# The last stage of a decoder layer, written in a fixed order: later statistics, kept weights, rows instead of columns

## The chip, the core and the metric

One core of a Trainium2 chip (trn2) runs the kernel. The time is device microseconds (us) of one execution; the figure to forecast is the median of such times. The engines are named as in the profile: PE (TensorE, matmuls), PEld (its weight load), DVE (VectorE), ACT (ScalarE), POOL (GpSimd), SP (SyncE, which issues all DMAs here).

## What is computed

One layer of a decoder on x of 1024 tokens by 1024 channels in f32: two token mixers, a SwiGLU block, and at its end a gated embedding and the final norm. The last stage of the kernel is these lines of the reference:

```python
    gate = jax.nn.sigmoid(rms_norm(x, norm_ple[i]) @ w_ple_gate[i])
    x = x + gate * (p[i] @ w_ple_proj[i])
return rms_norm(x, norm_final)
```

with `rms_norm(x, gain) = x * rsqrt(mean(x * x) + 1e-6) * gain`, the mean over a token's 1024 channels. All of it must hold to f32 accuracy.

## The kernel before

Activations lie transposed: a tile has 128 channels on the partitions and tokens in its columns, so x2 is eight tiles `x2[m]` of 128 x 1024. The tokens are worked in two halves of 512 columns, `hs(1)` first, then `hs(0)`. A product of f32 accuracy is made of three matmuls of rounded parts (`mm3`, L85 to L87): both operands are split into a high part (a cast on ScalarE, L105) and the rest (a subtraction on VectorE, L106). `xs3[m]` are the split tiles of x2 times the gain; `d_e[m]` in DRAM holds p W_pp, computed earlier.

The last stage begins at L996. For each half it makes eight products, one per output tile m: 24 matmuls against the eight `xs3` tiles into one PSUM bank. Each weight tile comes as two DMAs of 256 KB (`piece`), each of which is split (`halves`, a rotation of four pairs). A product is then finished in `finish` (L1011): times inv3 (L1014, DVE), sigmoid (L1015, ACT), times the tile `pe` loaded from d_e (L1016, DVE), added to x2 (L1017, DVE), squared (L596, L599, ACT) and summed into `acc` (L600, DVE).

A norm's factor is made from `acc` in `stat`: matmuls with a vector of ones sum over the partitions (L116), eleven small instructions on VectorE find the inverse root (L119 to L125), a diagonal is formed (L129), and one matmul spreads it over the partitions (`spread`, L141); ScalarE copies that to inv3 or inv4. There are four such factors of 512 tokens' width: inv3 of both halves at the start of the stage, inv4 of half 1, and inv4 of half 0, the last made in two quarters of 256 tokens at the very end.

Weights are loaded and split twice, once for each half. For the last two weight tiles of the second pass the product is made in quarters, `q2` and `q3`. The output of half 1 is scaled on VectorE (L1025) during the second pass; that of half 0 at the end, by the gain on ScalarE (L1055) and by inv4 on GpSimd and VectorE (`times`, L1059).

In this stage a scheduler sets the order of each engine's instructions. The stage before it (the down projection, L949 evacuates its PSUM banks, L109 and L110 make xs3) is written in a fixed order by `tc.manual_schedule`.

Of the kernel before, what the change touches and what calls it, by code (L numbers as in the profile page):

```python
# [43 lines left out]

@with_exitstack
def hybrid_block(ctx, tc, xT, pT, gains, pscale, w_u, w_qk, w_v, w_ga, w_gb, w_pool, w_a, w_b,
                 w_out, w_gate, w_up, w_down, w_pg, w_pp, out):
# [954 lines left out]
    inv4 = pp.tile([P, S], F32, name="inv4")  # L1002

    def ple_gate(m, w, sl):
        pe = pp.tile([P, HALF], F32, name="pe", bufs=3)[:, :sl.stop - sl.start]
        nc.sync.dma_start(pe, d_e[m][:, sl])
        pg = bank()[:, :sl.stop - sl.start]
        whole(pg, w, xs3, sl)
        return pg, pe

    def finish(m, pg, pe, sl):  # L1011
# [8 lines left out]
    def output(sl):  # L1020
        n = sl.stop - sl.start
        for c in range(0, KT, 2):
            o = pp.tile([P, 2 * HALF], F32, name="o", bufs=3)[:, :2 * n].rearrange("p (m n) -> p m n", m=2)
            for m in range(c, c + 2):
                nc.vector.scalar_tensor_tensor(o[:, m - c, :], x2[m][:, sl], gain(3, m), inv4[:, sl],  # L1025
                                               ALU.mult, ALU.mult)
            nc.sync.dma_start(out[c:c + 2, :, sl].rearrange("m p n -> p m n"), o)

    def squares(h):
        for m in range(KT):  # L1030
            square_into(acc, m, hs(h), nc.vector)

    def spread_into(inv, sl, dg):
        nc.scalar.copy(inv[:, sl], spread(psp, dg, (sl.stop - sl.start) // P))


    held = []
    for m in range(KT):
        w = pieces(w_pg[m])
        held.append((m, *ple_gate(m, w, hs(1))))  # L1040
        if m == 0:
            squares(1)
        elif m == 1:
            dg = stat(psp, acc[:, hs(1)], 4, ev())
            squares(0)
        elif m == 2:
            spread_into(inv3, hs(1), dg)
            dg = stat(psp, acc[:, hs(0)], 4, ev())
        elif m == 3:
            spread_into(inv3, hs(0), dg)  # L1050
        while m > 1 and held:
            finish(*held.pop(0), hs(1))

    def scale(m, sl):
        nc.scalar.activation(x2[m][:, sl], x2[m][:, sl], AF.Copy, scale=gain(3, m))  # L1055

    def times(c, n, sl, eng, inv):
        for m in range(c, c + n):
            eng.tensor_mul(x2[m][:, sl], x2[m][:, sl], inv)  # L1059
        nc.sync.dma_start(out[c:c + n, :, sl].rearrange("m p n -> p m n"), x2a[:, c:c + n, sl])  # L1060

    ws = []
    for m in range(KT):
        w = pieces(w_pg[m])
        if m < KT - 2:
            finish(m, *ple_gate(m, w, hs(0)), hs(0))
            scale(m, hs(0))
        else:
            ws.append((m, w))
        if m == 0:  # L1070
            dg = stat(psp, acc[:, hs(1)], 4, ev())
        if m == 1:
            spread_into(inv4, hs(1), dg)
            output(hs(1))
    q2, q3 = slice(0, 2 * P), slice(2 * P, HALF)
    for m, w in ws:
        finish(m, *ple_gate(m, w, q2), q2)
    (m, w), (m1, w1) = ws
    finish(m, *ple_gate(m, w, q3), q3)
    dg = stat(psp, acc[:, q2], 2, ev(2 * P))  # L1080
    finish(m1, *ple_gate(m1, w1, q3), q3)
    nc.scalar.copy(inv4[:, q2], spread(psp, dg, 2))
    dg = stat(psp, acc[:, q3], 2, ev(2 * P))
    for m, _ in ws:
        scale(m, q2)
    for c in (0, 4):
        times(c, 4, q2, nc.gpsimd, inv4[:, q2])
    for m, _ in ws:
        scale(m, q3)
    ps = spread(psp, dg, 2)  # L1090
    nc.scalar.copy(inv4[:, q3], ps)
    times(0, 2, q3, nc.gpsimd, inv4[:, q3])
    times(2, 3, q3, nc.vector, ps)
    times(5, 3, q3, nc.vector, ps)
# [46 lines left out]
```

## Time and profile before

| what | value |
|---|---|
| three runs | 1462.55, 1465.12, 1469.06 us; median 1465.12 |
| the profiled execution | 1468.2 us, span 1466.5 us |
| PE busy in the span | 1424.5 us (97%) |
| DVE, ACT, POOL busy | 1021.8, 630.6, 393.2 us (70%, 43%, 27%) |
| DMA | 221.73 MB, mean 151 GB/s |
| last stage, products of xs3 | 1347.4 to 1448.6 us |

Times in the rows below are microseconds from the start of the span. "busy" counts an engine's own instructions. A row of a timeline gives start, duration, engine, line, operation and names; in brackets stands how long the engine was idle before it and what ended that. Matmuls overlap, so two starts tell more than a duration.

### The profile page before, as it was taken

Reading aid. Unit: us, or ns where it says so; the run is one execution under the profiler, and the core shown is the slowest. Engines: PE = TensorE matmul, PEld = TensorE weight load, DVE = VectorE, ACT = ScalarE, POOL = GpSimd, SP = SyncE. Lnnn points to the kernel's source line nnn. Section 1 sums busy time; section 2 is a strip of 40 time slices with the busy share of each in tenths; the row PEclk is TensorE's granted clock in tenths of the full one; section 3 lists DMA queues with packets and bytes.
Section 4 is the critical chain, followed back from the end, with each engine's and each line's share of the span. In section 5 each row is a group of like instructions: output and inputs, shape, how many; then the busy total and the mean of one; then the engine's idle time right before and its main releaser. Section 6 shows DMA issues by size and latency. Waiting matters only on the chain.

```text
span 1466.5 us, 19073 instructions
## 1 busy us (share of the span) xinstructions
PE 1424.5 (97%) x6538; PEld 1170.6 (80%) x6538; DVE 1021.8 (70%) x1577; ACT 630.6 (43%) x1174; POOL 393.2 (27%) x454
## 2 busy tenths in 40 slices
PE   8999999999999999998899999999999999999995
PEld 7888888888888878886688888888887888887785
DVE  7680358888777777588656666666666777788886
ACT  6130455555555543355444444444443222226453
POOL 5000012333223300014424434444445233320001
PEclk9999999999999999999899999999999999999998
DMA  6131875455442168333234444444448466622352
GB/s 201 55 134 42 269 218 156 133 154 153 132 123 87 58 223 270 111 115 108 86 115 139 156 151 151 152 157 158 158 143 307 169 238 248 258 72 86 106 185 69
DMA packets 100656, 221.73 MB, mean 151 GB/s; under 512 B 10704, under 2 KB 22480, under 8 KB 100560
## 3 DMA queue, kind: packets, MB, share of 16 engines
q1 hardware_dynamic: 100560, 220.52, 45.2%
q8 instruction: 51, 0.84, 0.2%
q14 instruction: 45, 0.37, 0.1%
HBM read 151.80 MB, written 68.68 MB: 150 GB/s over the span
## 4 chain that ended last, share of the span: by engine, by line
PE 82%; DVE 8%; issue 6%; DMA 1%; POOL 1%; ACT 1%; SPq 0%; DVEq 0%; POOLq 0%; ACTq 0%
PE mm L87 25%; PE mm L86 25%; PE mm L85 25%; DVE fail L411 1%; PE pt L429 1%; DVE t L106 1%; DMA xt<-in_xT 1%; DVE wlo L106 1%; PE av L445 1%; PE av L444 1%; PE z L401 1%; PE z L402 1%; DVE ev L607 1%; PE mm L116 0%; PE mm L141 0%
## 5 line engine op out<-in xcount | busy, mean ns | idle before, releaser
L85 PE MATMUL mm<-t,whi 128*128 128x512 f32 x896 | 354.8, 396 | 9.1 <-ACT t L105 4.1
L105 ACT CAST whi<-wraw 128x512 fp32r<-128x512 f32 x316 | 193.8, 620 | 388.3 <-PE mm L86 264.6
L86 PE MATMUL mm<-t,whi 128*128 128x512 f32 x896 | 353.6, 395 | 4.1 <-DVE t L106 4.1
L87 PE MATMUL mm<-t,wlo 128*128 128x512 f32 x896 | 353.3, 395 | 2.0 <-DVE wlo L106 2.0
L106 DVE TENSOR_TENSOR wlo<-wraw,whi 128x512 fp32r<-128x512 f32 x316 | 233.5, 744 | 125.3 <-ACT whi L105 124.2
L85 PEld LDWEIGHTS mm<-t,whi 128*128 128x128 f32 x896 | 169.2, 189 | 53.0 <-ACT t L105 6.0
L86 PEld LDWEIGHTS mm<-t,whi 128*128 128x128 f32 x896 | 169.2, 189 | 43.6 <-DVE t L106 5.6
L87 PEld LDWEIGHTS mm<-t,wlo 128*128 128x128 f32 x896 | 169.1, 189 | 41.1 <-DVE wlo L106 2.8
L85 PE MATMUL mm<-xs,whi 128*128 128x512 f32 x384 | 154.6, 403 | 0.0
L87 PE MATMUL mm<-xs,wlo 128*128 128x512 f32 x384 | 150.3, 391 | 0.0
L86 PE MATMUL mm<-xs,whi 128*128 128x512 f32 x384 | 150.2, 391 | 0.0
L949 DVE TENSOR_TENSOR x<-mm,x 128x512 f32<-128x512 f32 x140 | 96.1, 690 | 42.8 <-PE mm L87 39.4
L106 DVE TENSOR_TENSOR t<-ev,t 128x512 fp32r<-128x512 f32 x91 | 89.9, 1010 | 30.7 <-ACT t L105 30.3
L411 DVE TENSOR_TENSOR_SCAN fail<-fail 128x1024 f32<-128x1024 f32 (+3 forms) x64 | 87.3, 1364 | 27.3 <-POOL fail L409 26.8
L695 POOL TENSOR_TENSOR ws<-wraw 128x512 f32<-128x512 f32 x22 | 29.9, 1357 | 283.5 <-DMA wraw<-in_w_gate 197.8
L105 ACT CAST t<-ev 128x512 fp32r<-128x512 f32 x95 | 57.5, 620 | 81.7 <-DVE ev L740 42.2
L105 ACT CAST ath<-pt 128x256 fp32r<-128x256 f32 (+1 forms) x176 | 54.8, 335 | 69.5 <-PE pt L429 38.8
L87 PEld LDWEIGHTS mm<-xs,wlo 128*128 128x128 f32 x384 | 72.1, 188 | 15.7
L85 PEld LDWEIGHTS mm<-xs,whi 128*128 128x128 f32 x384 | 72.2, 188 | 11.8 <-ACT sg L373 0.2
L86 PEld LDWEIGHTS mm<-xs,whi 128*128 128x128 f32 x384 | 72.3, 188 | 11.5
L409 POOL TENSOR_SCALAR_AFFINE_SELECT fail<-fail 128x128 f32<-128x128 f32 x64 | 20.6, 322 | 226.7 <-ACT fail L407 201.1
L106 DVE TENSOR_TENSOR atl<-pt,ath 128x256 fp32r<-128x256 f32 (+1 forms) x176 | 61.3, 367 | 18.1 <-ACT ath L105 17.8
(212 smaller groups left out, 2629.3 us busy)
## 6 DMA issues: line engine op xcount, KB each, us to landing
d_t<-t SPq DMA_DIRECT2D x36, 512.0 KB, 3.3
t<-d_t SPq DMA_DIRECT2D x36, 512.0 KB, 6.8
d_b<-t SPq DMA_DIRECT2D x27, 512.0 KB, 2.7
t<-d_b SPq DMA_DIRECT2D x27, 512.0 KB, 6.5
wraw<-in_w_gate SPq DMA_DIRECT2D x44, 256.0 KB, 2.7
wraw<-in_w_up SPq DMA_DIRECT2D x44, 256.0 KB, 3.0
wraw<-in_w_down SPq DMA_DIRECT2D x44, 256.0 KB, 5.1
wraw<-in_w_out SPq DMA_DIRECT2D x32, 256.0 KB, 3.1
```

The source lines that it names most:

```text
L85: nc.tensor.matmul(ps, w[0], x[0], start=first, stop=False, skip_group_check=onto)
L86: nc.tensor.matmul(ps, w[0], x[1], start=False, stop=False, skip_group_check=onto)
L87: nc.tensor.matmul(ps, w[1], x[0], start=False, stop=last, skip_group_check=onto)
L105: nc.scalar.copy(hi, src)
L106: (eng or nc.vector).tensor_sub(lo, src, hi)
L401: nc.tensor.matmul(zo, q[:, base:base + P], kh[:, ks], start=True, stop=False)
L402: nc.tensor.matmul(zo, q[:, base:base + P], kl[:, ks], start=False, stop=True)
L409: nc.gpsimd.affine_select(r[:, :P], r[:, :P], [[1, P]], ALU.is_gt, 1.0, base=0, channel_multiplier=-1)
L411: nc.vector.tensor_tensor_scan(r[:, :w], r[:, :w], r[:, :w], 1.0, ALU.mult, ALU.bypass)
L429: nc.tensor.transpose(pt[:, i, :], b[:, (c + i) * P:(c + i + 1) * P], ident)
L695: nc.gpsimd.tensor_add(s1, a21, a22)
L949: nc.vector.tensor_add(xx, ps, xx)
```

## The change

Only the last stage changes, and one helper: `inv_rms` takes a list of accumulators and sums them in PSUM. In the stage:

- Everything is written in one fixed order (`tc.manual_schedule` on all engines).
- The 16 products are numbered j = 0 to 15; j below 8 are tokens 512 to 1023. In the program's round j stand the product j on TensorE, the finishing of product j-1 (of two waiting products in j = 3 and 4), cut into three pieces by generators, and between these pieces the split of the weights of product j+1.
- The statistic of tokens 0 to 511 for inv3 moves from behind the products of m = 2 into product 6, and that of tokens 512 to 1023 stands in product 1, between two of its steps; the statistic for inv4 stands in product 9.
- The weights of m = 4 to 7 are split into tiles that are kept (`kh`, `kl`), so that the second pass loads and splits only m = 0 to 3.
- For tokens 0 to 511 no inv4 is spread. Their finished tiles are transposed on TensorE (`tokens`, 32 matmuls of 128 x 128), so that tokens lie on the partitions, and the eviction multiplies each row by its factor (`tokens_out`, five on ScalarE and three on VectorE). They go to a second output, `out_1`; the host puts both together.

```diff
+    wkp = ctx.enter_context(pool("wkp"))
+    KEEP = KT // 2
...
+    def prep(j, c):
+        m = j % KT
+        if j not in w:
+            w[j] = kept.get(m, [])
+        if len(w[j]) == 2:
+            return
+        raw = raws[j][c]
+        if m < KEEP:
+            pair = halves(raw)
+        else:
+            pair = [wkp.tile([P, HALF], F32R, name=f"{n}{m}{c}") for n in ("kh", "kl")]
+            split(*pair, raw)
+            kept.setdefault(m, w[j])
+        w[j].append(pair)
...
+    def finish(m, ps, pe, sl, sq=None):
...
+        nc.vector.tensor_mul(a, ps, inv3[:, sl])
         nc.scalar.activation(a, a, AF.Sigmoid)
+        yield
         nc.vector.tensor_mul(a, pe, a)
         nc.vector.tensor_add(x2[m][:, sl], x2[m][:, sl], a)
...
+        nc.scalar.activation(sq, x2[m][:, sl], AF.Square)
+        if sl.start < HALF:
+            nc.scalar.activation(x2[m][:, sl], x2[m][:, sl], AF.Copy, scale=gain(3, m))
+        yield
+        if 0 < m and not (m == KT - 1 and sl.start < HALF):
+            nc.vector.tensor_add(acc[:, sl], acc[:, sl], sq)
+        yield
...
+                nc.tensor.transpose(ps_of[t, m // 4][:, m % 4 * P:(m % 4 + 1) * P],
+                                    x2[m][:, t * P:(t + 1) * P], ident)
...
+        hooks = {1: {4: stat_at(31, acc[:, hs(1)], 4)}, 2: {1: spread_at(31, inv3[:, hs(1)])},
+                 6: {4: stat_at(30, acc[:, hs(0)], 4)}, 7: {1: spread_at(30, inv3[:, hs(0)])},
+                 9: {3: stat_at(41, acc[:, hs(1)], 4)}, 10: {1: spread_at(41, inv4)}}
+        for j in range(14):
+            m, sl = j % KT, hs(1 if j < KT else 0)
+            if j == 1:
+                squares(1, range(1, KT))
+            load_pe(j)
+            ps = products(j, sl, hooks.get(j, {}))
...
+            if j > 2:
+                todo = [waits.pop(0) for _ in range(min(len(waits), 2))]
+            f = [finish(*t) for t in todo]
+            waits.append((m, ps, pes[j], sl))
+            do(*f)
+            prep(j + 1, 0)
+            do(*f)
+            prep(j + 1, 1)
+            do(*f)
+            if 2 < j < 6:
+                squares(0, range(*((0, 3), (3, 6), (6, KT))[j - 3]))
+            if j + 3 < 2 * KT:
+                load(j + 3)
+            if j > 10 and j < 14:
+                output(((0,), (2,), (4, 6))[j - 11])
```

In the changed kernel the lines of a finish are L1049 (times inv3), L1050 (sigmoid), L1052 (times pe), L1053 (added to x2), L1056 (square), L1058 (gain) and L1061 (into acc); L1071 to L1075 are the squares of x2 before the stage, L118 and L122 to L132 the statistic, L144 the spread, L1086 the transposes, L1093 and L1095 the evictions.

Three places of the order follow. First ScalarE in the first pass, before. The names with `whi` are weights (the number before the half tells the raw tile: 12686 belongs to product 6, 12727 and 12733 to product 7), `ev_12528` to `ev_12625` are products 2 to 4.

```order
L1015 ACTIVATE ev_12528<-ev_12528 128x512
L105 CAST whi_12688<-wraw_12686 128x512
L599 ACTIVATE ev_12533<-x2_5854 128x512
L1015 ACTIVATE ev_12578<-ev_12578 128x512
L105 CAST whi_12729<-wraw_12727 128x512
L599 ACTIVATE ev_12583<-x2_5854 128x512
L1015 ACTIVATE ev_12625<-ev_12625 128x512
L105 CAST whi_12735<-wraw_12733 128x512
```

The same place on ScalarE now: `ev_12644` is product 4, `ev_12721` product 5; `kh60` and `kh61` are the halves of the weights of product 6, `kh70` and `kh71` of product 7; L1074 squares x2 for the statistic of tokens 0 to 511.

```order
L1050 ACTIVATE ev_12644<-ev_12644 128x512
L105 CAST kh60_12647<-wraw_12549 128x512
L1056 ACTIVATE ev_12653<-x2_5854 128x512
L105 CAST kh61_12655<-wraw_12551 128x512
L1074 ACTIVATE ev_12660<-x2_5854 128x512
L1074 ACTIVATE ev_12663<-x2_5854 128x512
L1050 ACTIVATE ev_12721<-ev_12721 128x512
L105 CAST kh70_12724<-wraw_12613 128x512
L1056 ACTIVATE ev_12730<-x2_5854 128x512
L105 CAST kh71_12732<-wraw_12615 128x512
```

Between the sigmoid of product m and its square stood a cast for product m+4 before; now a cast for product m+2 stands there, and the second one behind the square.

Second, VectorE at the first statistic of the stage, before: the subtractions that make the low weights of product 3 (`wlo_12539`, `wlo_12545`) and two additions into acc.

```order
L106 TENSOR_TENSOR wlo_12539<-wraw_12536,whi_12538 128x512
L600 TENSOR_TENSOR acc_12299<-acc_12299,ev_12357 128x512
L600 TENSOR_TENSOR acc_12299<-acc_12299,ev_12360 128x512
L106 TENSOR_TENSOR wlo_12545<-wraw_12542,whi_12544 128x512
L119 TENSOR_SCALAR nrm_a_12409<-mm_12404 128x4
L121 TENSOR_SCALAR nrm_y_12403<-nrm_a_12409 128x4
```

And VectorE at the statistic in product 6 now, from its last small instructions on; `kl70` and `kl71` are the low weights of product 7, `ev_12721` is product 5.

```order
L126 TENSOR_TENSOR nrm_t_12695<-nrm_a_12694,nrm_y_12688 128x4
L127 SCALAR_TENSOR_TENSOR nrm_t_12695<-nrm_t_12695,nrm_y_12688 128x4
L128 SCALAR_TENSOR_TENSOR nrm_y_12688<-nrm_t_12695,nrm_y_12688 128x4
L132 TENSOR_SCALAR ev_12707<-ident_66,nrm_y_12688 128x128 x4
L1049 TENSOR_TENSOR ev_12721<-mm_12619,inv3_12300 128x512
L106 TENSOR_TENSOR kl70_12725<-wraw_12613,kh70_12724 128x512
L1052 TENSOR_TENSOR ev_12721<-pe_12617,ev_12721 128x512
L1053 TENSOR_TENSOR x2_5854<-x2_5854,ev_12721 128x512
L106 TENSOR_TENSOR kl71_12733<-wraw_12615,kh71_12732 128x512
L1061 TENSOR_TENSOR acc_12299<-acc_12299,ev_12730 128x512
```

Before, the weights of product 3 were split ahead of the statistic that follows product 1; now the finish of product 5 and both subtractions for product 7 stand behind the statistic inside product 6.

Third, TensorE at the end, before: the last matmuls of the last product (m = 7, tokens 256 to 511), a spread, the last statistic and the last spread.

```order
L85 MATMUL mm_13254<-xsh7_11977,whi_13123 128x256
L86 MATMUL mm_13254<-xsl7_11978,whi_13123 128x256
L87 MATMUL mm_13254<-xsh7_11977,wlo_13124 128x256
L141 MATMUL mm_13287<-ev_13232,ones_62 128x256
L116 MATMUL mm_13292<-ones_62,acc_12299 128x1 x2
L141 MATMUL mm_13324<-ev_13290,ones_62 128x256
```

And now, from the last product's last matmuls; the first four groups of L1086 are tokens 0 to 255, the next tokens 256 to 511 without m = 7.

```order
L85 MATMUL mm_13180<-xsh7_11977,kh71_12732 128x256
L86 MATMUL mm_13180<-xsl7_11978,kh71_12732 128x256
L87 MATMUL mm_13180<-xsh7_11977,kl71_12733 128x256
L1086 MATMUL mm_13233<-ident_66,x2_5854 128x128 x4
L1086 MATMUL mm_13238<-ident_66,x2_5854 128x128 x4
L1086 MATMUL mm_13243<-ident_66,x2_5854 128x128 x4
L1086 MATMUL mm_13248<-ident_66,x2_5854 128x128 x4
L1086 MATMUL mm_13264<-ident_66,x2_5854 128x128 x4
L1086 MATMUL mm_13269<-ident_66,x2_5854 128x128 x3
L1086 MATMUL mm_13273<-ident_66,x2_5854 128x128 x4
L1086 MATMUL mm_13278<-ident_66,x2_5854 128x128 x3
L118 MATMUL mm_13286<-ones_62,acc_12299 128x1
```

Two spreads are gone, and 30 transposes stand ahead of the last statistic.

## Rows read from the trace of the kernel before

**Rows 1.** Windows of the last stage: start to end, length, then busy time of each engine, PEclk, DMA.

```profile
1347.40:1376.00 28.60, 25.78 (x105) 20.49 (x104) 24.33 (x60) 13.70 (x25) 0.00 (x0) 0.88 0.35 111
1376.00:1448.60 72.60, 72.09 (x364) 60.67 (x362) 61.21 (x120) 39.79 (x68) 0.00 (x0) 1.00 0.41 135
1448.60:1466.50 17.90, 2.69 (x10) 1.32 (x8) 9.17 (x26) 2.09 (x5) 7.32 (x10) 0.66 0.34 117
```

**Rows 2.** Timeline of PE in the last stage: statistics and single matmuls.

```profile
1358.85 1.05 PE L116 MATMUL mm<-ones,acc 128*128 128x1 f32 x8 [0.37 <-DVE acc L600]
...
1368.83 1.76 PE L116 MATMUL mm<-ones,acc 128*128 128x1 f32 x8 [2.45 <-DVE acc L600]
...
1371.45 0.63 PE L87 MATMUL mm<-xsh,wlo 128*128 128x512 f32 x1
1371.88 0.63 PE L85 MATMUL mm<-xsh,whi 128*128 128x512 f32 x1
...
1376.68 0.39 PE L86 MATMUL mm<-xsl,whi 128*128 128x512 f32 x1
1376.91 0.39 PE L87 MATMUL mm<-xsh,wlo 128*128 128x512 f32 x1
...
1452.35 0.61 PE L116 MATMUL mm<-ones,acc 128*128 128x1 f32 x4 [2.46 <-DVE acc L600]
```

**Rows 3.** Timeline of DVE and ACT, one tile's finish beside one split.

```profile
1401.34 0.69 DVE L1014 TENSOR_TENSOR ev<-mm,inv 128x512 f32<-128x512 f32 x1 [0.83 <-PE mm L87]
...
1402.07 0.63 ACT L1015 ACTIVATE ev<-ev 128x512 f32<-128x512 f32 x1 [0.29 <-DVE ev L1014]
1402.73 0.70 DVE L1016 TENSOR_TENSOR ev<-pe,ev 128x512 f32<-128x512 f32 x1
...
1403.46 0.69 DVE L1017 TENSOR_TENSOR x<-x,ev 128x512 f32<-128x512 f32 x1
1403.88 0.62 ACT L105 CAST whi<-wraw 128x512 fp32r<-128x512 f32 x1 [1.18 <-PE mm L86]
1404.40 0.63 ACT L599 ACTIVATE ev<-x 128x512 f32<-128x512 f32 x1
1404.53 0.69 DVE L106 TENSOR_TENSOR wlo<-wraw,whi 128x512 fp32r<-128x512 f32 x1 [0.38 <-ACT whi L105]
1405.14 0.69 DVE L600 TENSOR_TENSOR acc<-acc,ev 128x512 f32<-128x512 f32 x1
```

**Rows 4.** Timeline of ACT and DVE: table load, gain, output instructions.

```profile
1376.21 1.28 ACT L1015 ACT_TABLE_LOAD   x1
...
1410.79 0.63 ACT L596 ACTIVATE acc<-x 128x512 f32<-128x512 f32 x1
...
1411.45 0.72 ACT L1055 ACTIVATE x<-x,g_sb 128x512 f32<-128x512 f32 x1
...
1418.68 2.07 DVE L1025 SCALAR_TENSOR_TENSOR o<-x,g_sb,inv 128x512 f32<-128x512 f32 x3
```

**Rows 5.** Timeline of DVE behind the statistic at 1358.85: first and last instruction.

```profile
1359.94 0.16 DVE L119 TENSOR_SCALAR nrm_a<-mm 128x4 f32<-128x4 f32 x1 [0.27 <-PE mm L116]
...
1362.11 0.88 DVE L129 TENSOR_SCALAR ev<-ident,nrm_y 128x128 f32<-128x128 f32 x4
```

**Rows 6.** Timeline of ACT, DVE and POOL behind the last product.

```profile
1449.51 0.42 ACT L1015 ACTIVATE ev<-ev 128x256 f32<-128x256 f32 x1 [1.34 <-DVE ev L1014]
...
1449.96 0.43 DVE L1016 TENSOR_TENSOR ev<-pe,ev 128x256 f32<-128x256 f32 x1 [0.48 <-ACT ev L1015]
1450.38 5.91 POOL L1059 TENSOR_TENSOR x<-x,inv 128x256 f32<-128x256 f32 x8 [138.46 <-ACT inv L1082]
...
1453.62 0.64 DVE L123 TENSOR_TENSOR nrm_t<-nrm_a,nrm_y 128x2 f32<-128x2 f32 x1
```

**Rows 7.** Timeline of DVE: the last arithmetic of the kernel.

```profile
1459.52 2.08 DVE L1059 TENSOR_TENSOR x<-x,mm 128x256 f32<-128x256 f32 x6 [1.72 <-ACT inv L1091]
```

**Rows 8.** Timeline of PE in the attention stage: transposes.

```profile
206.49 1.03 PE L429 MATMUL pt<-ident,beta 128*128 128x128 f32 x8
```

More of the change, by code (lines that the diff above doesn't have):

```diff
@@ L113, in inv_rms @@
     def inv_rms(ps, acc, n, y):
+        accs = acc if isinstance(acc, list) else [acc]
         for t in range(n):
-            nc.tensor.matmul(ps[:, t:t + 1], acc[:, t * P:(t + 1) * P], ones[:, :1], start=True, stop=True)
+            for i, a in enumerate(accs):
+                nc.tensor.matmul(ps[:, t:t + 1], a[:, t * P:(t + 1) * P], ones[:, :1],
+                                 start=i == 0, stop=i == len(accs) - 1)
         a = const.tile([P, KT], F32, name="nrm_a", bufs=2)[:, :n]
@@ L941, in final @@
         split_gain(*part(xs3[m], hs(h)), x2[m][:, hs(h)], gain(2, m))
-    with tc.manual_schedule(engines={e.engine for e in (nc.tensor, nc.vector, nc.scalar, nc.gpsimd, nc.sync)}):
+    every = {e.engine for e in (nc.tensor, nc.vector, nc.scalar, nc.gpsimd, nc.sync)}
+    with tc.manual_schedule(engines=every):
         waiting = None
@@ L1001, in hybrid_block @@
     inv3 = pp.tile([P, S], F32, name="inv3")
[L1002 to L1011, printed above, removed]
+    inv4 = pp.tile([P, HALF], F32, name="inv4")
+    wkp = ctx.enter_context(pool("wkp"))
+    KEEP = KT // 2
+    q2, q3 = slice(0, 2 * P), slice(2 * P, HALF)
@@ new lines, in hybrid_block, with load, load_pe @@
+    kept, raws, pes = {}, {}, {}
+    def load(j):
+        m = j % KT
+        if j < KT or m < KEEP:
+            raws[j] = [piece(w_pg[m][:, hs(c)]) for c in range(2)]
+    def load_pe(j):
+        pes[j] = pp.tile([P, HALF], F32, name="pe", bufs=4)
+        nc.sync.dma_start(pes[j], d_e[j % KT][:, hs(1 if j < KT else 0)])
+    w = {}
+    def prep(j, c):
+        m = j % KT
+        if j not in w:
[10 more added lines that the diff above has]
+        w[j].append(pair)
@@ L1012, in finish, with gate_steps @@
+    def gate_steps(ps, j, sl):
+        for k in range(KT):
+            mm3(ps, col(w[j][k // 4], k % 4), part(xs3[k], sl), k == 0, k == KT - 1)
+            yield k
+    def finish(m, ps, pe, sl, sq=None):
         n = sl.stop - sl.start
         a = ev(n)
-        nc.vector.tensor_mul(a, pg, inv3[:, sl])
+        nc.vector.tensor_mul(a, ps, inv3[:, sl])
         nc.scalar.activation(a, a, AF.Sigmoid)
+        yield
         nc.vector.tensor_mul(a, pe, a)
         nc.vector.tensor_add(x2[m][:, sl], x2[m][:, sl], a)
-        square_into(acc, m, sl, nc.vector)
@@ L1020, in output @@
[L1020 to L1067, printed above, removed]
-        else:
[L1069 to L1094, printed above, removed]
+        if sq is None:
+            sq = acc[:, sl] if m == 0 else ev(n)
+        nc.scalar.activation(sq, x2[m][:, sl], AF.Square)
[4 more added lines that the diff above has]
+            nc.vector.tensor_add(acc[:, sl], acc[:, sl], sq)
@@ new lines, in finish, with do, squares, spread_into @@
+        yield
+    def do(*steps):
+        for x in steps:
+            next(x, None)
+    def squares(h, ms):
+        for m in ms:
+            if m == 0:
+                nc.scalar.activation(acc[:, hs(h)], x2[m][:, hs(h)], AF.Square)
+            else:
+                sq = ev()
+                nc.scalar.activation(sq, x2[m][:, hs(h)], AF.Square)
+                nc.vector.tensor_add(acc[:, hs(h)], acc[:, hs(h)], sq)
+    def spread_into(inv, dg):
+        nc.scalar.copy(inv, spread(psp, dg, 4))
@@ new lines, in tokens, with tokens_out @@
+    def tokens(ps_of, sl, ms):
+        for t in range(sl.start // P, sl.stop // P):
+            for m in ms:
+                if (t, m // 4) not in ps_of:
+                    ps_of[t, m // 4] = bank()
+                nc.tensor.transpose(ps_of[t, m // 4][:, m % 4 * P:(m % 4 + 1) * P],
+                                    x2[m][:, t * P:(t + 1) * P], ident)
+    def tokens_out(ps_of, y, t, c, eng):
+        o = ev()
+        i = t % 2
+        if eng is nc.scalar:
+            nc.scalar.activation(o, ps_of[t, c], AF.Copy, scale=y[:, i:i + 1])
+        else:
+            nc.vector.tensor_scalar(o, ps_of[t, c], y[:, i:i + 1], None, ALU.mult)
+        nc.sync.dma_start(outT[t][:, hs(c)], o)
@@ new lines, in hybrid_block, with products, stat_at, f @@
+    with tc.manual_schedule(engines=every):
+        load(0)
+        load(1)
+        for c in range(2):
+            prep(0, c)
+        load(2)
+        waits = []
+        rows = {}
+        def products(j, sl, hooks={}):
+            ps = bank()[:, :sl.stop - sl.start]
+            for k in gate_steps(ps, j, sl):
+                if k in hooks:
+                    hooks[k]()
+            return ps
+        state = {}
+        def stat_at(name, accs, n):
+            def f():
+                y = const.tile([P, KT], F32, name="nrm_y", bufs=2)[:, :n]
+                inv_rms(bank(), accs, n, y)
+                state[name] = y
+                if n == 4:
+                    dg = state[name, "dg"] = ev()
+                    diagonal(dg, y, 4)
+            return f
+        def spread_at(name, inv):
+            return lambda: spread_into(inv, state[name, "dg"])
+        def output(ms):
+            for c in ms:
+                o = pp.tile([P, 2, HALF], F32, name="o", bufs=2)
+                for m in range(c, c + 2):
+                    nc.vector.scalar_tensor_tensor(o[:, m - c, :], x2[m][:, hs(1)], gain(3, m), inv4, ALU.mult, ALU.mult)
+                nc.sync.dma_start(out[c:c + 2].rearrange("m p n -> p m n"), o)
+        hooks = {1: {4: stat_at(31, acc[:, hs(1)], 4)}, 2: {1: spread_at(31, inv3[:, hs(1)])},
[7 more added lines that the diff above has]
+            ps = products(j, sl, hooks.get(j, {}))
+            if j == 0:
+                squares(1, [0])
+            todo = []
+            if j > 2:
[13 more added lines that the diff above has]
+                output(((0,), (2,), (4, 6))[j - 11])
+        ps6, ps7 = {}, {}
+        sq = {}
+        def quarter(j, q, hooks={}):
+            return products(j, q, hooks)
+        def begin(m, ps, q):
+            if m == KT - 1:
+                sq[q.start] = ev(2 * P)
+            return finish(m, ps, pes[KT + m][:, q], q, sq.get(q.start) if m == KT - 1 else None)
+        load_pe(14)
+        load_pe(15)
+        f5 = [finish(*t) for t in waits]
+        prep(15, 0)
+        a2 = quarter(14, q2)
+        do(*f5)
+        do(*f5)
+        do(*f5)
+        b2 = quarter(15, q2)
+        f = begin(6, a2, q2)
+        do(f)
+        do(f)
+        do(f)
+        a3 = quarter(14, q3)
+        f = begin(7, b2, q2)
+        do(f)
+        do(f)
+        do(f)
+        b3 = quarter(15, q3, {2: stat_at(42, [acc[:, q2], sq[0]], 2)})
+        f = begin(6, a3, q3)
+        do(f)
+        do(f)
+        do(f)
+        o2, o3 = {}, {}
+        tokens(o2, q2, range(KT))
+        f = begin(7, b3, q3)
+        do(f)
+        tokens_out(o2, state[42], 0, 0, nc.scalar)
+        do(f)
+        tokens(o3, q3, range(KT - 1))
+        tokens_out(o2, state[42], 0, 1, nc.vector)
+        stat_at(43, [acc[:, q3], sq[2 * P]], 2)()
+        tokens(o3, q3, [KT - 1])
+        for c in range(2):
+            tokens_out(o2, state[42], 1, c, nc.scalar)
+        for t in (2, 3):
+            for c in range(2):
+                tokens_out(o3, state[43], t, c, (nc.vector, nc.scalar)[c])
```

10 lines of the change are left out of this document (6 added, 4 removed).

## The prediction

> **What bounds the kernel now.** Read first the table by stage [rows 1]. The last stage begins at 1347.4 us, where the first product with `xs3` starts, and its products end at 1448.6. In the middle stretch TensorE is busy 72.1 of 72.6 us at granted clock 1.00, with VectorE at 61.2 and ScalarE at 39.8: TensorE sets the pace, and VectorE has 15% to spare. Before it and behind it the table reads otherwise: clock 0.88 up to 1376, and 17.9 us behind the last product in which TensorE works 2.7 us.
>
> Next the timeline of TensorE [rows 2]. A statistic waits 0.37 us for `acc` at 1358.85. The next one waits 2.45 us at 1368.83, and behind it the matmuls start 0.43 us apart (1371.45, 1371.88), the 1.2 GHz level, until the 0.23 us of the 2.4 GHz level is back at 1376.7. At that level (0.227 us on the mean) a product of 24 matmuls takes 24 x 0.227 = 5.44 us.
>
> Then the two engines that carry a finished product on [rows 3]: multiply by inv3 (L1014, 1401.34), sigmoid 0.73 us later, times pe 0.66 later, added to x2 0.73 later. A cast is followed by the next ScalarE instruction after 0.52 us and by its subtraction after 0.65; independent VectorE instructions of 512 columns start 0.61 apart. I call these steps D = 0.61 (VectorE to VectorE, independent), DD = 0.73 (VectorE's result to anyone), A = 0.52 (ScalarE to ScalarE) and AD = 0.65 (ScalarE's result to VectorE).
>
> **Part by part.** *The statistics come later in the text, the work before the stage is untouched.* On VectorE 4 subtractions of weights instead of 7 stand ahead of the last addition into `acc` of tokens 512 to 1023; in the trace the statistic starts at 1358.85, so now at 1358.85 - 3 x 0.61 = 1357.0. The 2.45 us wait and the slow clock behind it go, since the second statistic moves to product 6. That is the gain: 2.45 and 12 matmuls x 0.2 = 2.4 us.
>
> *The order of ScalarE and VectorE.* This is the term that decides. In the change each round ties the split of product j+1 to the finishing of product j-1, in one fixed order on both engines: multiply, sigmoid, cast of half 0, subtraction, times pe, add, square, cast of half 1, subtraction, addition into acc. Neither engine can pass the other, so a round costs the sum of its steps: DD 0.73 + A 0.52 + AD 0.65 + D 0.61 + DD 0.73 + DD 0.73 + A 0.52 + AD 0.65 + D 0.61 + D 0.61 = 6.36 us, against 5.44 of TensorE. Before, the same instructions existed, but the cast beside the finishing of product m belonged to product m+4 (the order of ScalarE shows it), now to m+2. So nothing is left to cover the lag: TensorE must wait for the split. Rounds with more in them:
> - j=3 finishes two tiles, loads the sigmoid table (1.28 us, [rows 4]) and adds two squares: 0.73 + 1.28 + 0.52 + 0.52 + 0.65 + 0.61 + 0.73 + 0.61 + 0.73 + 0.73 + 0.52 + 0.65 + 0.61 + 3 x 0.61 = 10.7 us.
> - j=4 finishes two tiles and adds three squares of tokens 0 to 511: 0.61 + 0.73 + 0.52 + 0.65 + 0.61 + 0.73 + 0.61 + 0.73 + 0.73 + 0.52 + 0.65 + 0.61 + 5 x 0.61 = 10.7 us.
> - j=5: 6.36 and two additions, 7.6 us.
> - with the scaling by gain (0.66 behind the square, 0.72 long, as a step of the queue some 0.65; [rows 4]): 7.1 us, or 6.5 where m = 0 adds nothing to acc.
> - without a split but with two output instructions (0.69 each, [rows 4]): 5.4 us; with four 6.7; with none 4.1.
>
> *A statistic blocks VectorE.* nrm_a starts 1.09 us behind the first matmul of the statistic, 2.17 us later the diagonal begins, 0.88 us long [rows 2, 5]: 4.05 us. Now the multiply and the subtraction for the next product stand behind it in the queue (the order of VectorE shows it).
>
> *Walk along that chain.* Statistic at 1357.0; + 4.05 = 1361.1; then the subtraction for product 2 (0.7), the matmuls up to the spread (0.9), the spread (taken as a statistic, 1.0), the copy to inv3 (0.5), and cast and two subtractions for product 3 (0.65 + 1.2) bring the first multiply to 1366.1. Then j=3 to 1376.8, j=4 to 1387.5, j=5 to 1395.1; statistic, 1399.2; f5, f6, f7 at 6.36, 1418.3; statistic, 1422.3; f8 6.5 and f9 7.1, 1435.9; f10, f11 at 5.4, 1446.7; f12 6.7 and f13 4.1, 1457.5.
>
> *The quarters.* With 256 columns the steps are 0.45 us [rows 6], so a finish costs 2.6 us up to its addition and 2.25 up to its square: 1460.1 and 1462.4. The statistic of the first 256 tokens with its 11 small instructions costs 1.09 + 2.17 = 3.3, 1465.6; behind it in VectorE's queue both finishes of the second quarter, 1470.5; the last statistic 3.3, 1473.7; two evictions, 0.61 + 0.69, 1475.0. TensorE, kept waiting, ends its products near 1465.5 instead of 1448.6.
>
> *The tail.* Gone are two spreads, the inverse of a row of tokens, 10 multiplications on GpSimd (16 with VectorE's six, [rows 7]) and GpSimd beside VectorE: while it runs, small VectorE instructions take 0.64 us [rows 6] against 0.16 [rows 5]. Added are 32 transposes. The nearest row has 8 in 1.03 us [rows 8], 0.13 each; 14 of the last 16 stand ahead of the last statistic, 1.8 us, and are done while VectorE finishes the tile, so I cost them at nothing (1.8 us if that cover is gone). From the first matmul of the last statistic to the last arithmetic it is 1452.35 to 1461.6 now, 9.25 us ([rows 2, 7]), and 4.6 in the change: this part does gain 4.6 us. From there to the end of the span are 4.9 us of issues and landing [rows 1, 7]; eight transfers of 256 KB instead, the last four within 1.3 us, I leave at 4.9.
>
> *The kept weights* save 8 loads and 8 splits, in products 12 to 15. There VectorE and ScalarE are behind by the rounds above, so this shortens rounds (5.4 rather than 7.1), already in the walk; 2 MB fewer on SP's queue, where the weights of product j+3 are now issued in round j, 3 x 5.44 = 16 us ahead of their use, are worth nothing.
>
> **Sum.** 1475.0 + 4.9 = 1479.9 against 1466.5: +13.4 us. The clock: TensorE now waits over 2 us some four times (ahead of products 6, 7 and 10, and at the statistic in product 15). The wait of 2.45 us cost 2.4 us of slow clock [rows 2]; four would be 9.6 if nothing covered them, nothing at all where the two other engines set the end anyway. I take one, 2.4, since mostly the chain decides. Together +15.8; with the profiled execution's own 1468.2 us that is 1484.0. That execution lies 3.1 us above the median of the three runs, 1465.12, so the forecast of the median is **1481 us**, 1.1% slower. The walk's bounds are +9 (rounds j=3 and j=4 overlapping by 2 us each) and +23 (all slow clock uncovered). As a check of the prices, the queues of before walked in the same steps end the products at 1447.4, with 2.6 us of slow clock, where the trace has 1448.6.
>
> The Trainium skill, "VectorE: DVE Perf Modes", section "The DRAIN you can't avoid", says that the next VectorE instruction starts when the pipe is empty and that a semaphore between them costs nothing extra. By it the pair of pe and x2 in each of 18 finishes would cost D, not DD, 0.12 us less each and 2.2 us in all, 1479 us. The trace does not agree: 0.73 with the wait [rows 3], 0.61 without; I keep the trace.
>
> **Rivals.**
> 1. *Faster.* The rounds do not close into a chain: the splits come in time, as they do today, and only the work of TensorE counts. Its place is the start of each product from 5 on, and it decides if a round stays under 5.44 us. Then products take 336 x 0.227 + 96 x 0.12 = 87.8 us (0.12 an estimate for half the columns), three spreads and four statistics at 1.05 or less some 7 [rows 2], so they end at 1442.2 rather than 1448.6, -6.4; with 3 us less behind them 1456 us. For it: VectorE is busy 61 of 73 us and not full. Against it: the step rows add up to 6.36.
> 2. *No change.* Only the statistics hold TensorE: behind each the next product's subtraction is ready 4.05 + 0.61 + 0.65 us after its start, TensorE gets there after 1.0 for the statistic, 2.0 for nine matmuls and 0.5 for two more, so 1.8 us each, three times 5.4, and the backlog of j=3 to 5 adds 4 to 8 us, while the rounds of 6.36 are caught up by the lighter ones from j=10. That gives 1462 to 1470.
> 3. *Slower still.* The transposes are the end. The row has eight of them between other products; 32 alone behind waits may run at the lower level, 0.26 each, and the 30 ahead of the last statistic would take 7.8 us from 1465.5, 1473.3 instead of 1470.5; with the four slow stretches uncovered 1488 and more. [...] No run here shows transposes alone.
>
> **Chances.** Forecast 0.74, rival 1 0.05, rival 2 0.13, rival 3 0.08. The range takes rival 2 from its upper third and the bounds of the walk: 1469 to 1489. A measurement tells about 0.5% from no change, 7.3 us: faster 0.05, same (up to 1472.4) 0.14, slower 0.81.
>
> **What would show it.** Right: TensorE waits in products 5 to 7 and 10 for ScalarE's cast or VectorE's subtraction, rounds of over 6 us between two multiplies of L1049, products ending near 1465, and a last statistic of under 5 us to the last eviction. Wrong: if L1049 comes every 5.4 us from product 6 on, or if products end before 1455, the chain is not closed and my step prices are too long.

## The result, and the profile after

Median 1484.26 us (four runs, 1483.05 to 1486.86) against 1466.85 of the kernel before on the same chip: ratio 1.0122, 95% interval 1.0101 to 1.0143, so 1.2% slower; the forecast was 1481 us. The profiled execution is one of 1483.05 us with a span of 1481.3.

The windows of the last stage (columns as in [rows 1]):

```profile
1347.00:1376.00 29.00, 27.13 (x120) 21.49 (x119) 20.77 (x44) 14.89 (x26) 0.00 (x0) 1.00 0.34 108
1376.00:1448.60 72.60, 61.92 (x240) 45.38 (x239) 46.86 (x95) 26.34 (x45) 0.00 (x0) 0.93 0.21 69
1448.60:1468.50 19.90, 16.51 (x113) 15.87 (x112) 12.71 (x32) 7.08 (x13) 0.00 (x0) 0.86 0.36 120
1468.50:1481.30 12.80, 5.11 (x42) 4.87 (x40) 6.10 (x20) 5.27 (x10) 0.00 (x0) 0.77 0.44 164
```

In the same 72.6 us TensorE began 364 matmuls before [rows 1] and begins 240 now. None of the three engines is full: TensorE is busy 61.9 of the 72.6 us, VectorE 46.9 against 61.2 before. So no engine has too much work; they wait for each other. The products with `xs3` start at 1346.67, 0.7 us earlier than in the profile of before, and the last one starts its last matmul at 1468.31, 20 us later than before, and what stands behind them has shrunk from 17.9 to 12.8 us.

Whom TensorE waits for, its timeline:

```profile
1379.57 0.50 PE L85 MATMUL mm<-xsh,kh 128*128 128x512 f32 x1 [1.05 <-ACT kh L105]
...
1390.19 0.50 PE L85 MATMUL mm<-xsh,kh 128*128 128x512 f32 x1 [2.75 <-ACT kh L105]
...
1402.16 0.79 PE L85 MATMUL mm<-xsh,kh 128*128 128x512 f32 x1 [2.78 <-ACT kh L105]
...
1425.59 0.50 PE L85 MATMUL mm<-xsh,whi 128*128 128x512 f32 x1 [2.04 <-ACT whi L105]
...
1463.87 0.58 PE L118 MATMUL mm<-ones,ev 128*128 128x1 f32 x2 [1.77 <-ACT ev L1056]
```

In four of these rows it waits for the cast of a weight, which depends on nothing but a landed raw tile and, where tiles rotate, a free one; in the last row, inside the statistic of the first 256 tokens, it waits for a square. The casts are late because of where they stand, as experiment 1 will show. One round, VectorE first, then ScalarE:

```profile
1400.20 0.68 DVE L1049 TENSOR_TENSOR ev<-mm,inv 128x512 f32<-128x512 f32 x1
1402.14 0.69 DVE L106 TENSOR_TENSOR kl<-wraw,kh 128x512 fp32r<-128x512 f32 x1 [1.26 <-ACT kh L105]
1402.75 0.69 DVE L1052 TENSOR_TENSOR ev<-pe,ev 128x512 f32<-128x512 f32 x1
1403.47 0.69 DVE L1053 TENSOR_TENSOR x<-x,ev 128x512 f32<-128x512 f32 x1
1405.43 0.69 DVE L106 TENSOR_TENSOR kl<-wraw,kh 128x512 fp32r<-128x512 f32 x1 [1.26 <-DMA wraw<-in_w_pg]
1406.04 0.68 DVE L1061 TENSOR_TENSOR acc<-acc,ev 128x512 f32<-128x512 f32 x1
1406.64 0.68 DVE L1049 TENSOR_TENSOR ev<-mm,inv 128x512 f32<-128x512 f32 x1
```

```profile
1400.97 0.63 ACT L1050 ACTIVATE ev<-ev 128x512 f32<-128x512 f32 x1 [6.56 <-DVE ev L1049]
1401.51 0.60 ACT L105 CAST kh<-wraw 128x512 fp32r<-128x512 f32 x1
1404.26 0.63 ACT L1056 ACTIVATE ev<-x 128x512 f32<-128x512 f32 x1 [2.15 <-DVE x L1053]
1404.79 0.60 ACT L105 CAST kh<-wraw 128x512 fp32r<-128x512 f32 x1
```

Read both by start times: 1400.20 multiply, 1400.97 sigmoid, 1401.51 cast, 1402.14 subtraction, 1402.75, 1403.47, 1404.26 square, 1404.79 cast, 1405.43 subtraction, 1406.04 addition, 1406.64 next multiply. Each starts 0.53 to 0.79 us after its predecessor on the other engine or on its own, and none starts ahead of it. That is 6.44 us for a round, where a product takes 5.44. The row at 1405.43 names a DMA as releaser, but its raw tile had already been read by the cast at 1404.79: the subtraction waits for that cast, 0.64 us earlier.

The tail, TensorE, then ScalarE and VectorE:

```profile
1468.52 4.03 PE L1086 MATMUL mm<-ident,x 128*128 128x128 f32 x30
1472.38 0.28 PE L118 MATMUL mm<-ones,acc 128*128 128x1 f32 x2
```

```profile
1471.82 0.42 ACT L1056 ACTIVATE ev<-x 128x256 f32<-128x256 f32 x1 [0.37 <-DVE x L1053]
...
1475.53 1.41 DVE L1095 TENSOR_SCALAR ev<-mm,nrm_y 128x512 f32<-128x512 f32 x2
```

From the last statistic to the last arithmetic it is 1472.38 to 1476.94, 4.56 us, against 9.25 before [rows 2, 7].

### The profile page after: what moved, and what is told of

The parts are those of the page before. It is cut to its first block, busy times and chain, and to the rows that moved or that the text cites. A ratio compares the mean times of both kernels' runs of the same rounds, so it can differ in the third digit from the quotient of the medians.

```text
span 1481.3 us, 19060 instructions
## 1 busy us (share of the span) xinstructions
PE 1434.4 (97%) x6574; PEld 1174.8 (79%) x6574; DVE 1013.1 (68%) x1560; ACT 627.2 (42%) x1169; POOL 386.7 (26%) x444
## 4 chain that ended last, share of the span: by engine, by line
PE 76%; DVE 11%; issue 7%; ACT 2%; DMA 2%; POOL 1%; SPq 0%; DVEq 0%; POOLq 0%; ACTq 0%
PE mm L87 24%; PE mm L86 24%; PE mm L85 24%; DVE fail L414 1%; PE pt L432 1%; DVE t L106 1%; DVE wlo L106 1%; PE av L448 1%; PE av L447 1%; PE z L404 1%; PE z L405 1%; DVE ev L610 1%; DVE x L953 1%; DMA xt<-in_xT 1%; DMA wraw<-in_w_down 1%
## 5 line engine op out<-in xcount | busy, mean ns | idle before, releaser
L105 ACT CAST whi<-wraw 128x512 fp32r<-128x512 f32 x300 | 183.7, 620 | 361.0 <-PE mm L86 247.3
L106 DVE TENSOR_TENSOR wlo<-wraw,whi 128x512 fp32r<-128x512 f32 x300 | 223.9, 752 | 136.2 <-ACT whi L105 134.8
```

Source lines behind the costliest of these rows:

```text
L105: nc.scalar.copy(hi, src)
L106: (eng or nc.vector).tensor_sub(lo, src, hi)
```

## The experiments

My theory is called "closed round" in what follows: the order inside a round ties both engines into one chain of ten steps. Each ratio is to the kernel before, timed on the same chip.

**1. Casts ahead of the sigmoid.** The same instructions, in another order within the round (`prep` only casts here, and `subs` holds the subtractions):

```diff
+            [prep(j + 1, c) for c in range(2)]
             do(*f)
-            prep(j + 1, 0)
+            [nc.vector.tensor_sub(b, raw, a) for (a, b), raw in subs]; subs.clear()
             do(*f)
-            prep(j + 1, 1)
             do(*f)
```

> The changed kernel (1484 us) with one thing reordered: in each round both casts of the next product's weights stand ahead of the sigmoid on ScalarE, and both subtractions between the multiply by inv3 and the multiply by pe on VectorE. Same instructions, same tiles. Closed round (my theory): the casts leave the chain, a round without gain then costs 0.73 + 1.1 (two subtractions and what is left of the sigmoid's shade) + 0.73 + 0.73 + 0.65 + 0.61 = 4.6 us, under the 5.44 us of a product; walked through the queues the last arithmetic comes 18 us earlier, 1464 to 1468 us, and L1049 comes every 5.4 us from product 6 on. Late split (rival: only that a split belongs to the very next product matters, not the order inside a round): the split still belongs to the next product, so 1480 to 1485. Statistics (rival: only the blocks behind the statistics hold TensorE): 1480 to 1485. Tail (rival: transposes and the half clock at the end): unchanged, 1484.

Measured 1468.93 us, ratio 1.0025 (1.0014 to 1.0037). VectorE, one round:

```profile
1397.42 0.69 DVE L1049 TENSOR_TENSOR ev<-mm,inv 128x512 f32<-128x512 f32 x1
1398.03 1.28 DVE L1154 TENSOR_TENSOR wlo<-wraw,whi 128x512 fp32r<-128x512 f32 x2
1399.23 0.69 DVE L1052 TENSOR_TENSOR ev<-pe,ev 128x512 f32<-128x512 f32 x1
1399.95 0.69 DVE L1053 TENSOR_TENSOR x<-x,ev 128x512 f32<-128x512 f32 x1
1401.34 0.70 DVE L1061 TENSOR_TENSOR acc<-acc,ev 128x512 f32<-128x512 f32 x1 [0.70 <-ACT ev L1056]
1401.95 0.68 DVE L1049 TENSOR_TENSOR ev<-mm,inv 128x512 f32<-128x512 f32 x1
```

Both subtractions lie where VectorE waited for the sigmoid; the round is 4.53 us, as summed, and TensorE waits for no cast; beside the statistics it only waits 1.1 and 1.0 us, each time for a subtraction that stands behind one. The loads are issued as in the change, so weights that land late were not the cause of its waits there. (Rounds then follow TensorE's products, except where one catches up, as here.) By the ratios it came out some 14 us below the change (1.0025 against 1.0122), not 18, and so just above the 1464 to 1468 expected: the last product still waits 1.76 us for a square inside a statistic, and the last 14 matmuls behind it start 0.21 us apart in place of 0.12.

**2. Splits two products ahead**, the order inside a round untouched (not shown: the tiles that this needs, named in the expectation, and the split of product 1, now ahead of the first round):

```diff
-            prep(j + 1, 0)
+            prep(j + 2, 0)
             do(*f)
-            prep(j + 1, 1)
+            prep(j + 2, 1)
```

> The changed kernel with the splits one product further ahead (the weights of product j+2 in round j; a third pair of tiles for m = 2, and three weight tiles kept instead of four, which makes one split more). The order of steps inside a round is untouched. Closed round: TensorE gets the splits early, but the ten steps on ScalarE and VectorE still add up to 6.4 us a round, so the finishes fall behind and the end stays: 1482 to 1487; TensorE then waits in long pieces at the statistics (about 9 us in product 6, 6 in product 9, 6 in product 15) in place of the many waits for casts. Late split: TensorE no longer waits and the loss is gone, 1466 to 1470. Statistics: the subtractions now stand ahead of them, 1478 to 1480. Tail: unchanged.

Measured 1486.2 us, ratio 1.014 (1.0117 to 1.0164): no gain. No matmul waits for a cast any more, the rounds are 6.44 and 6.39 us again, and TensorE now stands at the statistics:

```profile
1396.66 1.87 PE L118 MATMUL mm<-ones,acc 128*128 128x1 f32 x8 [8.60 <-DVE acc L1075]
...
1420.94 1.87 PE L118 MATMUL mm<-ones,acc 128*128 128x1 f32 x8 [3.34 <-DVE acc L1061]
```

This run decides between my theory and "late split", which wanted 1466 to 1470. The wait moved; the end did not. My later waits were too large (3.3 and 3.5 us where I had 6), the first was right.

**3. One cast moved.** The two lines `prep(j + 1, 1)` and the second `do(*f)` change places, so the second cast stands directly behind the first.

> The changed kernel with half of the reordering: only the second cast and its subtraction move ahead of the multiply by pe, the first stays where it was. Closed round: the steps between two multiplies by inv3 are then 0.73 (multiply) + 0.52 (sigmoid) + 0.52 (first cast) + 0.65 (second cast) + 0.61 + 0.73 + 0.73 + 0.65 (square) + 0.61 = 5.75 us, between the 6.4 of the change and the 4.55 with both casts ahead, and still above the 5.44 of a product; rounds of the middle at 5.75 to 5.85, last arithmetic 5.7 us earlier, 1477 to 1480 us. Late split or statistics: no difference to the change, 1483 to 1486.

Measured 1479.73 us, ratio 1.0083 (1.0062 to 1.0104), between the two as expected. VectorE's multiplies:

```profile
1398.04 0.68 DVE L1049 TENSOR_TENSOR ev<-mm,inv 128x512 f32<-128x512 f32 x1
1403.98 0.68 DVE L1049 TENSOR_TENSOR ev<-mm,inv 128x512 f32<-128x512 f32 x1
1409.98 0.68 DVE L1049 TENSOR_TENSOR ev<-mm,inv 128x512 f32<-128x512 f32 x1
```

Rounds of 5.94 and 6.00 us, a little over the 5.75 to 5.85 of the sum.

**4. The scheduler's order.** One line, and the whole text of the stage is left to the scheduler:

```diff
-    with tc.manual_schedule(engines=every):
+    if True:
```

> The changed kernel with its last stage given to the scheduler instead of a written order: same instructions, kept tiles, statistics' places in the text and tail. The order it gives puts casts two to four products ahead. Closed round: ScalarE and VectorE are no longer tied, TensorE waits at the first statistic (3.0 us) and its spread (2.1), has a slow stretch behind that, and runs through; last arithmetic about 1456 to 1458 in the span, 1461 to 1466 us. Statistics: the blocks behind statistics remain, 1475 to 1484. Tail: unchanged, 1484.

Measured 1462.6 us, ratio 0.9967 (0.9951 to 0.9983). The window that held 240 matmuls holds 365, TensorE busy all the time:

```profile
1376.00:1448.60 72.60, 72.60 (x365) 60.57 (x364) 56.11 (x114) 31.75 (x55) 0.00 (x0) 1.00 0.22 73
```

So some 22 us of the change are its order, and without it the rest of the change is a small gain. I had foreseen a wait of 2.1 us at the spread too; the trace has only the one at the statistic.

**5. No kept weights**, in three orders: `KEEP = KT`, so that all 16 products split theirs. First the change itself:

> The changed kernel without kept weights: all 16 products load and split theirs. Closed round: the rounds 11 to 14 get back their casts and subtractions, 7.1 instead of 5.4 us and more where outputs stand in them; walked through the queues the last arithmetic comes 10 us later, 1493 to 1496. Late split: four more products wait for their split, 1.5 to 2.5 us each, 1490 to 1494. Statistics or tail: splits are hidden beside TensorE, 1484 to 1486.

Measured 1492.61 us, ratio 1.0188 (1.0161 to 1.0215), just under my range and inside that of "late split", so the time does not part the two; the rounds, at the price of the sum, speak for mine. VectorE's multiplies in the second pass:

```profile
1437.40 0.69 DVE L1049 TENSOR_TENSOR ev<-mm,inv 128x512 f32<-128x512 f32 x1
1445.81 0.68 DVE L1049 TENSOR_TENSOR ev<-mm,inv 128x512 f32<-128x512 f32 x1
1454.22 0.69 DVE L1049 TENSOR_TENSOR ev<-mm,inv 128x512 f32<-128x512 f32 x1
```

8.41 us a round, which is 7.1 with gain and split and two outputs of 0.66; in the change the same rounds take 5.43 (1437.25 to 1442.68). Then with the casts ahead, as in experiment 1:

> Casts ahead of the sigmoid, and no kept weights (all 16 products load and split theirs). Closed round: a split now lies mostly in the shade of the finish, but the rounds of products 10 to 13 hold gain, output and two subtractions at once, 5.9 to 6.5 us against 5.44, so kept weights are worth 4 to 5 us here against the 8.3 us that they were worth in the order of the change: 1472 to 1475. If kept weights are worth the same in any order: 1477. If they are worth nothing once the order is mended: 1468 to 1470.

Measured 1473.79 us, ratio 1.0038 (1.0022 to 1.0053). The chip was another than in experiment 1, so both were timed again side by side:

> The reordered kernel again, on the same chip as the next one, since the two were timed on different chips and their ratios to the kernel before (1.0025 and 1.0038) differ by less than their medians do. 1467 to 1470 us.

> The reordered kernel without kept weights. Closed round: 4 to 5 us above the one with kept weights, from the rounds of products 10 to 13. If splits are worth nothing once the order is mended: within 1.5 us of it.

Measured 1469.08 and 1472.79 us, ratios 1.0005 (0.9992 to 1.0017) and 1.0036 (1.0023 to 1.0049): kept weights are worth 3 to 5 us there. And left to the scheduler:

> The last stage given to the scheduler, and no kept weights. Closed round: with nothing tied, the 8 splits more are hidden beside TensorE; and since kept tiles need no free rotation, the scheduler had put four casts and subtractions of theirs ahead of the first statistic, which go away: the first statistic waits 1 us less, last arithmetic 1 to 3 us earlier than with kept weights, 1459 to 1462. If splits cost the products anything: 1466 to 1470.

Measured 1457.33 us, ratio 0.9932 (0.9914 to 0.9951), the fastest of all, some 5 us below experiment 4 (on another chip, so by the ratios) and below the 1459 to 1462 that I expected. The first statistic there and here:

```profile
1363.81 1.05 PE L118 MATMUL mm<-ones,acc 128*128 128x1 f32 x8 [2.56 <-DVE acc L1075]
```

```profile
1359.84 1.05 PE L118 MATMUL mm<-ones,acc 128*128 128x1 f32 x8 [0.59 <-DVE acc L1075]
```

With kept tiles the scheduler had put some of their casts and subtractions ahead of that statistic. The wait is 2.0 us shorter, not the 1 us of my sum, and the matmuls behind the long one start 0.43 us apart for some eight starts, which those behind the short one do not. The same saved splits are thus worth about 9 us, 4 us or minus 5, by the order they stand in. (From the first product of the stage to the end of the span, in one profiled execution of each, they are worth 8.8, 2.8 and minus 4.5 us.)

**6. The transposes.** The 14 of tokens 256 to 511 behind the last statistic:

```diff
-        tokens(o3, q3, range(KT - 1))
         tokens_out(o2, state[42], 0, 1, nc.vector)
         stat_at(43, [acc[:, q3], sq[2 * P]], 2)()
-        tokens(o3, q3, [KT - 1])
+        tokens(o3, q3, range(KT))
```

> The changed kernel with the 14 transposes of tokens 256 to 511 moved from ahead of the last statistic to behind it. Closed round: the transposes are covered by the finish of the last tile, whose square is what the last statistic waits for, and the 16 now behind it are covered by its small instructions: 1483 to 1485. Tail: the statistic starts 14 transposes, 1.9 us, earlier: 1482, and the last arithmetic in the span comes 1.5 to 2 us earlier.

Measured 1484.26 us, ratio 1.0118 (1.0094 to 1.0143): no difference. TensorE:

```profile
1468.28 2.11 PE L1086 MATMUL mm<-ident,x 128*128 128x128 f32 x16
1470.22 0.28 PE L118 MATMUL mm<-ones,acc 128*128 128x1 f32 x2
1472.04 0.38 PE L118 MATMUL mm<-ones,ev 128*128 128x1 f32 x2 [1.54 <-ACT ev L1056]
```

The statistic is there two us earlier and then waits for the square. The transposes are covered, as costed.

**7. The tail alone**, in the kernel before (scheduler, no kept weights): from the quarters on its text is replaced by `tokens`, `tokens_out` and a statistic without diagonal, and neither spread nor GpSimd is left in the tail.

> The kernel before, with its scheduler and without kept weights, and only the new tail: transposes on TensorE, eviction scaled by rows, second output, no spread, nothing on GpSimd. My sum for the tail: from the first matmul of the last statistic to the last arithmetic 4.6 us in place of 9.25, so 4 to 5 us faster than before, 1460 to 1462. Tail (rival): 30 transposes at 0.26 us ahead of the last statistic eat that gain, 1465 to 1468.

Measured 1460.3 us, ratio 0.9954 (0.9935 to 0.9972). TensorE, and VectorE's last row:

```profile
1444.92 3.44 PE L1082 MATMUL mm<-ident,x 128*128 128x128 f32 x30
1448.19 0.50 PE L116 MATMUL mm<-ones,acc 128*128 128x1 f32 x4
```

```profile
1450.90 1.41 DVE L1091 TENSOR_SCALAR ev<-mm,nrm_y 128x512 f32<-128x512 f32 x2
```

1448.19 to 1452.31 is 4.1 us in place of 9.25. The tail is a gain by itself, 4 to 9.5 us by the interval.

**8. Casts ahead, and the tail's finishes side by side** (`g = [begin(6, a2, q2), begin(7, b2, q2)]` and the same for q3, stepped together; the statistic of the first 256 tokens moved out of the last product to behind it).

> Casts ahead of the sigmoid as in the reordered kernel, and the two quarter tiles of m = 6 and 7 finished side by side, with the statistic of tokens 0 to 255 behind the products instead of inside the last one. Closed round: with no wait for that statistic there is no slow clock in the last product, products end at 1443 in the span, last arithmetic at 1455, 1459 to 1462 us, faster than the kernel before by 0.3%. Tail: the transposes at the lower clock remain, 1464 to 1467.

Measured 1466.63 us, ratio 0.9997 (0.9986 to 1.0008): 5 us short of what I expected. Against experiment 1 the ratios do not settle it, since that kernel had 1.0025 and, in its repeat, 1.0005; from the first product of the stage to the end of the span the profiled executions take 117.1 us here and 120.3 and 120.2 there. The time lies in the range of "tail", but not for its reason: the transposes start 0.11 us apart behind the first of each group, at the upper level. The last product indeed runs at full clock, but the products end at 1449.7 and not 1443. What I had left out, in TensorE's timeline:

```profile
1390.64 1.05 PE L118 MATMUL mm<-ones,acc 128*128 128x1 f32 x8 [1.78 <-DVE acc L1075]
...
1392.46 0.63 PE L85 MATMUL mm<-xsh,kh 128*128 128x512 f32 x1
1392.89 0.63 PE L86 MATMUL mm<-xsl,kh 128*128 128x512 f32 x1
...
1415.54 0.50 PE L87 MATMUL mm<-xsh,wlo 128*128 128x512 f32 x1 [1.02 <-DVE wlo L1154]
```

Behind the statistic's wait the matmuls start 0.43 us apart, the 1.2 GHz level, for eight starts (1.6 us), and two subtractions that stand behind statistics on VectorE hold TensorE 1.0 and 1.1 us; with a stage that starts 0.45 us later in this execution and a wait at this statistic 0.4 us longer than in my walk (not shown here), that is 4.5 of the 6.7 us. The rest I did not trace.

## Why the prediction was right

**The order** was the term that decides, and the runs show it: reordering inside the round takes it away (1), half the reordering takes about a third of it (3), more lookahead none (2), and the scheduler's order all (4). The prices held: rounds 6.44 and 6.39 us for 6.36; with gain 6.48 and 7.09 for 6.5 and 7.1; with two outputs 5.43 for 5.4, with four 6.76 for 6.7, with none 4.10 for 4.1. The statistic's block is 1396.14 to 1400.20, 4.06 for 4.05. One thing I put wrongly: that the cast belongs to the next product but one is not what closes the round. It only decides where TensorE's wait shows. Experiment 2 gave the splits a product more and lost as much.

**The double rounds** were mis-sized: 10.98 and 11.50 us for 10.7 each. In the second, five additions into acc took 3.52 us (1384.70 to 1388.22), 0.47 more than my 0.61 for each, the price of independent instructions:

```profile
1384.70 1.41 DVE L1061 TENSOR_TENSOR acc<-acc,ev 128x512 f32<-128x512 f32 x2
1386.03 2.28 DVE L1075 TENSOR_TENSOR acc<-acc,ev 128x512 f32<-128x512 f32 x3
```

The two groups write different halves of acc. Inside a group each reads what the last one wrote, and the steps are 0.72, 0.79 and 0.80 us; the two steps out of a group are 0.61 and 0.61. The other 0.3 us of this round I did not trace.

**The slow clock** was a wrong term. I took one fall on the path, 2.4 us. The trace has three stretches of it (granted clock 0.66 in 1390 to 1395, 0.55 in 1402 to 1409, and the last product), behind waits of 2.75, 2.78 and 1.77 us; the wait of 2.04 us ahead of product 10 has none (1.00 in 1425.5 to 1430). But the round of 1400.20 to 1406.64 lies in one and takes its 6.44 us, and the last multiply (1470.00) starts behind VectorE's own addition, 1.5 us after the last product. On that path only the statistic of the first 256 tokens was lengthened, by about 0.4 us. The products end at 1468.5 and not 1465.5, since this statistic came 1.5 us late and the 15 matmuls behind it start 0.21 us apart in place of 0.12. That the sum came out is luck, since other terms were short: last arithmetic 1476.94 against 1475.0 without the clock term, and 4.4 us behind it against 4.9. With that term the walk's span is 1482.3, measured 1481.3. The forecast of 1481 us for the median still was 3.3 us low, because I took off 3.1 us for a profiled execution above its median; the one of the change lies 1.2 below its own.

**The first statistic** started at 1356.49 (1357.0 foreseen; 1.6 us sooner after the start of the stage than before, for 1.8), and the wait of 2.45 us at the second [rows 2] is gone with its slow clock, as costed. **The tail** gave 4.56 for 4.6 us, with the transposes at nothing. **The kept weights** shorten rounds, as in the walk: 8.41 to 5.43.

**The rivals.** *Faster* is what experiment 4 comes near (1462.6 against 1456): for the written order it failed on the sum of the steps. *No change*, in which only the statistics hold TensorE, fell with experiments 1 and 2: by it 1480 to 1485 and 1478 to 1480 us, measured 1469 and 1486. *Slower still* fell with experiments 6 and 7: the transposes ahead of the last statistic cost nothing, and 30 take 3.44 us in experiment 7, at granted clock 1.00. Here they take 4.03 us, and the clock rises in their midst (two windows, columns as in [rows 1], and the durations of the transposes in ns, least, median and most):

```profile
1468.50:1469.70 1.20, 1.20 (x8) 1.20 (x7) 0.68 (x3) 0.46 (x2) 0.00 (x0) 0.50 0.00 0
1470.00:1471.00 1.00, 1.00 (x12) 1.00 (x11) 0.52 (x3) 0.72 (x3) 0.00 (x0) 1.00 0.00 0
L1086 PE MATMUL mm<-ident,x x32: 272/273/421, 1468.5 to 1473.3; 128*128 128x128 f32 x32
```

At 0.50 they start 0.21 us apart, at 1.00 0.11. So the rival had a transpose at the lower level nearly right (0.26), but only the first six ran there; and my 0.13, 1.03 us over eight, counted in the last one's full duration. One transpose lasts 273 ns (the median above), which agrees with the about 275 ns that the Trainium skill, "TensorE: Matmul & The Clock Gate", Part 4, gives; that is a duration, and back to back the next one starts before it is over. By the Trainium skill's "VectorE: DVE Perf Modes", section "The DRAIN you can't avoid", a wait between two VectorE instructions costs nothing extra. The trace does not agree here either: 1402.75 to 1403.47 is 0.72 us with the dependence, 1402.14 to 1402.75 is 0.61 without.

## What to carry to other kernels

When instructions of two in-order engines are written by hand, add the steps from one instruction to its next turn, through both queues, and compare that sum with the engine that should set the pace; busy shares (65% and 36% here) don't show it. If the round is too long, more lookahead only moves the wait: put independent work where an engine waits for the other one. And time a saving in the order it will stand in: the same eight splits were worth about 9, 4 or minus 5 us.

## What was not expected of the hardware

An addition into a tile half that the instruction ahead of it wrote starts 0.72 to 0.80 us behind that one, where independent ones stand 0.61 apart.

How long TensorE waited does not tell by itself whether the clock falls behind the wait. In experiment 8 a wait of 1.78 us was followed by eight starts 0.43 us apart; in experiment 3 a wait of 3.29 us was followed by none, at granted clock 1.00 (the wait, and a window with the columns of [rows 1]):

```profile
1388.55 0.50 PE L85 MATMUL mm<-xsh,kh 128*128 128x512 f32 x1 [3.29 <-ACT kh L105]
1388.50:1392.50 4.00, 3.95 (x15) 2.66 (x15) 3.24 (x6) 1.84 (x4) 0.00 (x0) 1.00 0.46 145
```

And in experiment 5, with the casts ahead (1473.79 us), the lower level came behind a wait of 1.02 us:

```profile
1455.79 0.38 PE L118 MATMUL mm<-ones,ev 128*128 128x1 f32 x2 [1.02 <-ACT ev L1056]
1457.00:1459.50 2.50, 2.50 (x14) 2.50 (x13) 1.80 (x11) 0.35 (x1) 0.00 (x0) 0.50 0.02 7
```

What decides it stays open here.

Transposes of 128 x 128 feel the clock like other matmuls: 0.21 us apart at granted clock 0.50, 0.11 at 1.00.
